# Seven block products in place of eight for two of eight pairs of feature tiles in the down projections

## The chip, the cores and the metric

The kernel runs on one core of a Trainium2 chip. The engines used are TensorE (PE: matmuls, and PEld for the loads of their stationary operand), VectorE (DVE), ScalarE (ACT), GpSimd (POOL, almost idle) and SyncE (SP), whose queue issues the loads of the weights. Each engine works through its own queue in a fixed order, and semaphores hold an instruction back until its inputs are there and its output buffer is free. The metric is the time of one execution on the device in microseconds; less is better.

## What is computed

A two-layer decoder trunk in float32, 256 tokens of 2048 features: a gated short convolution, an MLP, shared keys and values, stick-breaking attention, a second MLP. Only the MLPs matter here; each stands between two norms and is added to the residual:

```python
D_MODEL = 2048; SEQ = 256; D_FF = 4 * D_MODEL

def sq_relu_mlp(u, w_up, w_down):
    return jnp.square(jax.nn.relu(u @ w_up)) @ w_down

def reference(...):
    ...
    u = rmsnorm(h, mlp_pre_g[i])
    h = h + rmsnorm(sq_relu_mlp(u, mlp_w_up[i], mlp_w_down[i]), mlp_post_g[i])
    ...
```

## The kernel before

**Two-part numbers.** TensorE multiplies float32 operands in a rounded format (F32R). To keep accuracy, every operand is split into a high part (the rounded value) and a low part (the rest), and a product is the sum of three matmuls: high x high, high x low of the weights, low of the activations x high (lines 258 to 260). For each weight chunk ACT writes the high part (L149) and DVE the low part (L160; with a gain L162).

**Chunks and buffers.** All weights come as one stream of chunks of 128 x 1024, 512 KB each. `load_one` (L125) issues a chunk's load on SP's queue into one of 4 raw buffers (`RAW`), `split_one` (L177) splits it into a pair of tiles `hi` and `lo`, of which there are rings of 7 each (`RING`), and issues the next load. `chunk(i)` (L187) is called when TensorE's work on chunk i is written down, and sees to it that splits up to `i + 4` (`AHEAD`) are written down first.

**Who sets the order.** TensorE's order is that of the program's text. For DVE and ACT the compiler's planner picks the order: of what is ready it takes the piece of the highest priority, as a rule the one written earlier; `high_priority` puts a piece ahead. Some stretches are ordered by hand for DVE and ACT (`manual_schedule`): the ends of the sub-layers, where a projection's last results pass through the norm into the next sub-layer. They begin with `leave.begin()` in `run` (L293) and end some units later. The class `Norms` and its kinds `KeyNorms` (end of the first MLP) and `OutNorms` (end of the second) say what is done there; the results go through `post`, `gained`, `residual`, `input` and `enter` (transposing on TensorE, L211).

**The MLP** (`mlp`, L774) works in four quarters of the hidden features. A quarter `up(q)` computes 16 feature tiles of 128 x 256 tokens; `hidden` (L778) takes each from PSUM, applies the squared ReLU and splits the tile into high and low (`split_tile`, L201). Up tile n uses PSUM bank `(n + 2) % 8`. Then the quarter's down projection adds its share: two groups j of 1024 output columns each, 16 chunks to a group, one for each of the 16 feature tiles.

**A group** (`Group`, L240) has 2 token blocks b x 2 column halves c, four PSUM banks (2 to 5 for j = 0; 6, 7, 0 and 1 for j = 1). For every chunk `unit(b, i)` issues, for both halves, the three matmuls of 512 columns (`half`, L248): 12 matmuls a chunk. After the last chunk `evict` takes the four banks: in the first quarter a copy on ACT (L854), later a sum on DVE into `part` (L857); in the last quarter `after.post` follows. At the end of an MLP `run` stops the regular order `edge` chunks early (4 for `KeyNorms`, 6 for `OutNorms`), and `last_units` (L270) takes the remaining chunks for one bank after the other, so that the four results come one at a time.

`[P, 512]` scratch comes from `dump` (tag `sq`), gained inputs from the tag `hg` (4 buffers), the gain row of the norm ahead of the MLP from the tag `gpre` (one buffer of 128 x 2048), results from `result` (8 buffers).

Of the kernel before, what the change touches and what calls it, by code (L numbers as in the profile page):

```python
# [9 lines left out]
F32 = mybir.dt.float32  # L10
F32R = mybir.dt.float32r
AF = mybir.ActivationFunctionType
ALU = mybir.AluOpType
# [31 lines left out]
WARM = 8  # L45
LATER = 7
QUARTERS = FF // D

IN_N = [j * KD + i for i in range(KD) for j in range(3)]

# [15 lines left out]
def trunk(ctx, tc, x, xT, vecs, rows, ws, out):  # L66
# [39 lines left out]
    def bank(i, name):  # L106
        return psum.tile([P, 512], F32, tag=f"b{i}", name=name)
# [13 lines left out]
    last_load = [None]  # L121
    count = {"loaded": 0, "split": 0, "limit": 1 << 30, "apart": False}
    lows = []

    def load_one():  # L125
        i = count["loaded"]
# [16 lines left out]
    def high_parts(i):  # L143
        while count["loaded"] <= i:
            load_one()
        hi = wsplit.tile([P, CW], F32R, tag="hi", name=f"whi{i}")
        lo = wsplit.tile([P, CW], F32R, tag="lo", name=f"wlo{i}")
        for j, (at, gain) in enumerate(pieces_of(i)):
            rounded = nc.scalar.activation(  # L149
                hi[:, at], raw[i][:, at], AF.Copy, scale=1.0 if gain is None else gain  # L150
            )
# [14 lines left out]
    def low_parts(until=None):  # L166

        while lows and (until is None or lows[0] <= until):
# [5 lines left out]
            if until is None:  # L174
                break

    def split_one():  # L177
        i = count["split"]
        high_parts(i)
# [60 lines left out]
    class Group:  # L240
# [21 lines left out]
        def unit(self, b, i):  # L262
# [4 lines left out]
                    self.evict(b, c, self.ps.pop((b, c)))  # L267
            spent(UNIT)

        def last_units(self, b, edge):  # L270

            for c in range(2):
                for i in range(self.n - edge, self.n):
                    self.half(b, c, i)
                    if i == self.n - 1:
                        self.evict(b, c, self.ps.pop((b, c)))
                    spent(UNIT / 2)

    def run(groups, enter=False, leave=None):

        units = [(gr, i) for gr in groups for i in range(gr.n)]
        first, last = EDGE if enter else 0, len(units) - (leave.edge if leave else 0)
        for b in range(NB):
            for gr, i in units[:first]:
                gr.unit(b, i)
        for gr, i in units[first:last]:
            if i == 0 and gr.start is not None:
                gr.start()
            for b in range(NB):
                gr.unit(b, i)  # L290
# [465 lines left out]
        y = convolution(tmp)  # L756


    def project(w, xs, n_groups, evict, shift=0):
        groups = []  # L760
        for j in range(n_groups):
            banks = [[(4 * j + 2 * b + c + shift) % 8 for c in range(2)] for b in range(NB)]
# [11 lines left out]
    def mlp(pool, i, before, after):  # L774
        u = before.x4
        part = [[None] * 4 for _ in range(NB)]

        def hidden(xs, n, ps):  # L778
# [9 lines left out]
        def up(q, xs):  # L788
            w = W["up", i, q]
            order = UP_FIRST if q == 0 else UP_ORDER  # L790
            place = {kn: m for m, kn in enumerate(order)}
            pss = {}

            def high(k, n, b=None, begin=True, end=False):

                if n not in pss:
                    pss[n] = bank((n + 2) % 8, "up")
                ps, x = pss[n][:].rearrange("p (a b t) -> p a b t", a=2, b=NB), u[k // 4][:, k % 4]
                if b is None:
                    nc.tensor.matmul(  # L800
                        ps, weight(0, k, n), x, start=begin and k == 0, stop=end and k == KD - 1, skip_group_check=end
                    )
                else:
                    nc.tensor.matmul(ps[:, :, b, :], weight(0, k, n), x[:, :, b, :], start=k == 0 and b == 0, stop=False)  # L804
                if end and k == KD - 1:
                    hidden(xs, n, pss.pop(n))
                spent(TILE_HIGH if b is None else TILE_LOW)

            def low(k, n, begin=False, end=True):
                if n not in pss:  # L810
                    pss[n] = bank((n + 2) % 8, "up")
                x = u[k // 4][:, k % 4, 0].rearrange("p b t -> p (b t)")
                nc.tensor.matmul(  # L813
                    pss[n][:, :T], weight(1, k, n), x, start=begin and k == 0, stop=end and k == KD - 1,
                    skip_group_check=begin,
                )
                if end and k == KD - 1:
                    hidden(xs, n, pss.pop(n))
# [12 lines left out]
            lead = list(range(LEAD_UP if q == 0 else 0))  # L831
            if lead:
                first = [(k, n) for k in range(ALONE) for n in lead]
                for b in range(NB):
                    for k, n in sorted(first, key=lambda kn: (kn[0] // 4, kn[1] // 3 if kn[0] < 4 else 0)):
                        high(k, n, b)
                for k, n in first:
                    low(k, n)
                for k in range(ALONE, KD):
                    tiles_of([(k, n) for n in lead])  # L840
            for n in range(len(lead), KD):
                if n % 2 == 0:
                    tiles_of([(k, n) for k in range(KD)])
                else:
                    for k in range(KD):
                        low(k, n, True, False)
                    for k in range(KD):
                        high(k, n, None, False, True)

        def add(q):  # L850
            def evict(b, c, ps):
                if q == 0:
                    part[b][c] = result()
                    nc.scalar.activation(part[b][c], ps[:], AF.Copy)  # L854
                    return
                with tc.high_priority():
                    nc.vector.tensor_tensor(part[b][c], part[b][c], ps[:], op=ALU.add)  # L857
                if q == QUARTERS - 1:
                    after.post(b, c, part[b][c], part[b][c], before.hs[b][:])
            return evict  # L860

        for q in range(QUARTERS):
            xs = [None] * 4
            up(q, xs)
            if q == QUARTERS - 1:
                turned["banks"] = [2, 3]
            run(project(W["dn", i, q], xs, 2, add(q), 2), leave=after if q == QUARTERS - 1 else None)
# [262 lines left out]
```

## Time and profile before

| | |
|---|---|
| median of 3 runs | 2177.99 us (2177.91 to 2178.13) |
| the profiled execution | 2177.66 us |
| its span, first to last instruction | 2175.9 us |
| mean granted TensorE clock | 0.999 of full |
| busy: PE, PEld, DVE, ACT | 2165.6, 1854.0, 1341.7, 1128.3 us |
| loads of `w_dn` | 256 of 512 KB, 4.0 us to landing |
| first and last matmul of the down projections (L258) | 454.1 and 2166.8 us |

All views come from one profiled execution. The page has the busy time of each engine, the span in 40 slices, the DMA queues, the chain that ended last (followed back from the last instruction to whatever released it), and the costliest groups of instructions. Beside the page the trace answers by line and shape (groups), by who waited for whom (waits), in order of time (timeline; in brackets the engine's idle time before a row and what ended it), and by stage (windows: each engine's busy time in a stretch). Matmuls overlap in the pipeline, so the length of one is not its price; the distance between starts is. L258 is line 258 of the kernel.

### The profile page before, as it was taken

How to read it: one execution, taken by the hardware profiler on the slowest of the kernel's cores; microseconds unless marked ns; L12 is line 12 of the kernel's file. 1: busy time of each engine (PE TensorE's matmuls, PEld its weight loads, DVE VectorE, ACT ScalarE, POOL GpSimd, SP SyncE). 2: the span in 40 equal slices, each digit the busy share in tenths (PEclk: the TensorE clock that was granted, in tenths of full speed). 3: DMA queues.
4: the chain of work that ended last, by engine and by line, in shares of the span. 5: the costliest groups of instructions: out<-in, count | busy, mean ns of one | idle time of the engine just before them, and what ended most of it. 6: DMA issues, size and time to landing. Idle time of an engine off the chain costs nothing.

```text
span 2175.9 us, 28843 instructions
## 1 busy us (share of the span) xinstructions
PE 2165.6 (100%) x11074; PEld 1854.0 (85%) x11074; DVE 1341.7 (62%) x1835; ACT 1128.3 (52%) x1530; POOL 4.4 (0%) x13
## 2 busy tenths in 40 slices
PE   9999999999999999999999999999999999999998
PEld 8888888888888888888888888889888888888886
DVE  8766656854654664565666777558545645655655
ACT  7544444644543453454467888446445434544543
POOL 0000000000000000000000000000000000000000
PEclk9999999999999999999999999999999999999999
DMA  8666575666566666656575546656666666666663
GB/s 304 211 193 193 187 231 165 219 196 193 184 195 193 193 188 195 192 187 185 154 227 163 155 155 208 191 163 220 195 194 186 193 195 192 192 191 193 188 194 116
DMA packets 114762, 417.18 MB, mean 192 GB/s; under 512 B 12864, under 2 KB 13120, under 8 KB 113600
## 3 DMA queue, kind: packets, MB, share of 16 engines
q1 hardware_dynamic: 113472, 408.65, 60.5%
q0 software_dynamic: 864, 6.29, 0.8%
q8 instruction: 87, 1.43, 0.3%
q14 instruction: 51, 0.42, 0.1%
q10 hardware_dynamic: 288, 0.39, 0.1%
HBM read 413.19 MB, written 2.10 MB: 191 GB/s over the span
## 4 chain that ended last, share of the span: by engine, by line
PE 98%; ACT 1%; DMA 0%; DVE 0%; issue 0%; SPq 0%; DVEq 0%; ACTq 0%
PE up L800 20%; PE acc L258 17%; PE acc L260 17%; PE acc L259 17%; PE up L813 11%; PE acc L662 11%; PE lead L662 2%; PE up L804 1%; PE tr L211 1%; PE z L909 0%; PE o L957 0%; ACT whi L149 0%; DMA raw<-w_in 0%; DMA raw<-w_v 0%; ACT L902 0%
## 5 line engine op out<-in xcount | busy, mean ns | idle before, releaser
L160 DVE TENSOR_TENSOR wlo<-raw,whi 128x1024 fp32r<-128x1024 f32 (+1 forms) x678 | 815.7, 1214 | 654.4 <-ACT whi L149 537.8
L149 ACT ACTIVATE whi<-raw 128x1024 fp32r<-128x1024 f32 (+1 forms) x678 | 711.5, 1051 | 642.6 <-PE acc L260 452.9
L800 PE MATMUL up<-u,whi 128*128 128x512 f32 x1952 | 458.3, 390 | 0.0
L800 PEld LDWEIGHTS up<-u,whi 128*128 128x128 f32 x1952 | 361.6, 188 | 71.8
L258 PE MATMUL acc<-whi,hid 128*128 128x512 f32 x1024 | 398.4, 389 | 0.0
L260 PE MATMUL acc<-whi,hid 128*128 128x512 f32 x1024 | 398.4, 389 | 0.0
L259 PE MATMUL acc<-wlo,hid 128*128 128x512 f32 x1024 | 398.3, 389 | 0.0
L813 PEld LDWEIGHTS up<-u,wlo 128*128 128x128 f32 x2048 | 256.0, 191 | 5.8
L813 PE MATMUL up<-u,wlo 128*128 128x256 f32 x2048 | 259.0, 283 | 0.0
L259 PEld LDWEIGHTS acc<-wlo,hid 128*128 128x128 f32 x1024 | 192.2, 188 | 40.0
L260 PEld LDWEIGHTS acc<-whi,hid 128*128 128x128 f32 x1024 | 192.2, 188 | 40.0
L258 PEld LDWEIGHTS acc<-whi,hid 128*128 128x128 f32 x1024 | 192.2, 188 | 39.8
L162 DVE SCALAR_TENSOR_TENSOR wlo<-raw,gv,whi 128x512 fp32r<-128x512 f32 (+1 forms) x160 | 132.1, 854 | 43.7 <-ACT whi L149 43.1
L662 PE MATMUL acc<-u,whi 128*128 128x512 f32 x672 | 156.5, 390 | 0.0
L258 PE MATMUL acc<-whi,u 128*128 128x512 f32 x384 | 153.1, 399 | 0.1
L260 PE MATMUL acc<-whi,u 128*128 128x512 f32 x384 | 149.9, 390 | 0.0
L259 PE MATMUL acc<-wlo,u 128*128 128x512 f32 x384 | 149.7, 390 | 0.0
L149 ACT ACTIVATE whi<-raw,gv 128x512 fp32r<-128x512 f32 (+1 forms) x160 | 121.8, 801 | 51.6 <-PE acc L260 38.9
L662 PEld LDWEIGHTS acc<-u,whi 128*128 128x128 f32 x672 | 124.7, 188 | 25.0
L205 ACT ACTIVATE hid<-s 128x256 fp32r<-128x256 f32 x128 | 52.9, 418 | 106.9 <-DVE s L783 106.4
L780 ACT ACTIVATE half<-up 128x256 f32<-128x256 f32 x128 | 48.3, 382 | 93.2 <-PE up L813 49.2
L260 PEld LDWEIGHTS acc<-whi,u 128*128 128x128 f32 x384 | 72.1, 188 | 15.5
(144 smaller groups left out, 1681.5 us busy)
## 6 DMA issues: line engine op xcount, KB each, us to landing
raw<-w_up SPq DMA_DIRECT2D x256, 512.0 KB, 3.9
raw<-w_dn SPq DMA_DIRECT2D x256, 512.0 KB, 4.0
raw<-w_in SPq DMA_DIRECT2D x94, 512.0 KB, 4.0
raw<-w_out SPq DMA_DIRECT2D x32, 512.0 KB, 4.4
raw<-w_v SPq DMA_DIRECT2D x32, 512.0 KB, 4.4
raw<-w_k SPq DMA_DIRECT2D x32, 512.0 KB, 4.2
raw<-w_q SPq DMA_DIRECT2D x32, 512.0 KB, 4.1
raw<-w_wo SPq DMA_DIRECT2D x32, 512.0 KB, 3.6
```

What stands on the lines that cost most here:

```text
L149: rounded = nc.scalar.activation(hi[:, at], raw[i][:, at], AF.Copy, scale=1.0 if gain is None else gain)
L160: nc.vector.tensor_tensor(lo[:, at], t[:, at], hi[:, at].bitcast(F32), op=ALU.subtract)
L162: nc.vector.scalar_tensor_tensor(lo[:, at], t[:, at], gain, hi[:, at].bitcast(F32), op0=ALU.mult, op1=ALU.subtract)
L205: nc.scalar.activation(hi, src, AF.Copy)
L211: nc.tensor.transpose(to[:, j * P : (j + 1) * P], src[:, j * P : (j + 1) * P], ident[:])
L258: nc.tensor.matmul(ps[:], xh, hi[:, a], start=i == 0 and k == 0, stop=False)
L259: nc.tensor.matmul(ps[:], xh, lo[:, a], start=False, stop=False)
L260: nc.tensor.matmul(ps[:], xl, hi[:, a], start=False, stop=i == self.n - 1 and k == self.ks - 1)
L662: nc.tensor.matmul(ps[:, :cols], w, xs[:, :cols], start=k == 0 and part == parts[0], stop=k == KD - 1 and part == parts[1], skip_group_che ...
L780: nc.scalar.activation(half[:], ps[:, T:], AF.Copy)
L800: nc.tensor.matmul(ps, weight(0, k, n), x, start=begin and k == 0, stop=end and k == KD - 1, skip_group_check=end)
L813: nc.tensor.matmul(pss[n][:, :T], weight(1, k, n), x, start=begin and k == 0, stop=end and k == KD - 1, skip_group_check=begin,)
```

## The change

In each group the feature tiles form eight pairs (0, 1), (2, 3), ..., and for two of them, (2, 3) and (8, 9), the products are formed in another way (`PAIRS`). For a pair the activations are a 2 x 2 block matrix A (two token blocks by two feature tiles), the weights a 2 x 2 block matrix B (two feature tiles by two column halves), and the group needs A B added to its four banks. Before: eight block products, three matmuls each. After: seven block products (Winograd's form of Strassen's method), three matmuls each, whose operands are partly sums: four sums of activations s1 to s4, four of weights t1 to t4. Four of the seven products are added up over both pairs in four further PSUM banks, three go straight to the group's banks; after the second pair the four banks are combined and added to the results.

- `split_seven` takes the place of two splits: four subtractions on DVE, then high and low parts of four tiles in the rings `hi` and `lo` (a: 512 columns, b, t and u: 1024 each).
- `sums_of`, called from `hidden` after tiles 3 and 9, forms s1 to s4 on DVE and splits them; both groups of the quarter use them.
- `Mixed.seven` issues the 21 matmuls; the second tile of a pair issues none.
- `combined` takes the four banks: one copy on ACT and eight sums on DVE; in the first quarter four sums, which start `part`, so that the group's own eviction is a sum on DVE in every quarter.
- The sums of weights and the combining share one buffer under the tag `gpre`; the sums of activations lie under `hg` and `sq`.
- The group's banks stay as they were; the four others are those of the other group of the quarter.

```diff
+PAIRS = (2, 8)
...
+    def split_seven(i):
+
+        while count["loaded"] <= i + 1:
+            load_one()
+        a, b = raw.pop(i), raw.pop(i + 1)
+        sums = sevens[i].tile([P, 4, HALF], F32, tag="gpre", name="sums", bufs=1)
+        t1, t2, t3, t4 = (sums[:, j, :] for j in range(4))
+        b11, b12, b21, b22 = a[:, :HALF], a[:, HALF:], b[:, :HALF], b[:, HALF:]
+        for t, x, y in ((t1, b12, b11), (t3, b22, b12), (t2, b22, t1), (t4, b21, t2)):
+            nc.vector.tensor_tensor(t, x, y, op=ALU.subtract)
+        factors = []
+        for name, src in (("a", b11), ("b", b[:]), ("t", sums[:, 0:2, :]), ("u", sums[:, 2:4, :])):
+            n = 1 if name == "a" else 2
+            src = src if n == 1 or name == "b" else src.rearrange("p a b -> p (a b)")
+            hi = wsplit.tile([P, CW], F32R, tag="hi", name=f"whi{i}{name}")
+            lo = wsplit.tile([P, CW], F32R, tag="lo", name=f"wlo{i}{name}")
+            at = slice(0, n * HALF)
+            nc.scalar.activation(hi[:, at], src, AF.Copy)
+            low_part(hi, lo, src, at, None)
+            factors += [(hi[:, j * HALF : (j + 1) * HALF], lo[:, j * HALF : (j + 1) * HALF]) for j in range(n)]
+        parts[i] = factors
+        count["split"] += 2
+        load_one()
+        load_one()
...
+        def both(self, i):
+            if i in PAIRS:
+                self.seven(i)
+            elif i - 1 not in PAIRS:
+                super().both(i)
+
+        def seven(self, i):
+            b11, b21, b22, t1, t2, t3, t4 = chunk(self.first + i)
+            if self.more is None:
+                self.more = [bank(n, "more") for n in self.extra]
+            sh, sl = self.sums[i]
...
+            p1, p5, p6, p7 = self.more
+            for ps, (xh, xl), (hi, lo), own in (
+                (p1, x(0, 0), b11, True), (self.ps[0, 0], x(1, 0), b21, False), (self.ps[0, 1], sums(3), b22, False),
+                (p5, sums(0), t1, True), (p6, sums(1), t2, True), (p7, sums(2), t3, True),
+                (self.ps[1, 0], x(1, 1), t4, False),
+            ):
+                nc.tensor.matmul(ps[:], xh, hi, start=own and i == PAIRS[0], stop=False)
+                nc.tensor.matmul(ps[:], xh, lo, start=False, stop=False)
+                nc.tensor.matmul(ps[:], xl, hi, start=False, stop=own and i == PAIRS[-1])
+            if i == PAIRS[-1]:
+                self.combine(*self.more)
...
+        def sums_of(x, y):
+
+            t = after.dump()
+            s1, s2, s3, s4 = (t[:, j * P : (j + 1) * P] for j in range(4))
+            a11, a21, a12, a22 = x[:, :P], x[:, P:], y[:, :P], y[:, P:]
+            for to, u, v, op in (
+                (s1, a21, a22, ALU.add), (s2, s1, a11, ALU.subtract),
+                (s3, a11, a21, ALU.subtract), (s4, a12, s2, ALU.subtract),
+            ):
+                nc.vector.tensor_tensor(to, u, v, op=op)
+            hi, lo = (pool.tile([P, 512], F32R, tag="hg", name="sums", bufs=4) for _ in range(2))
+            nc.scalar.activation(hi[:], t[:], AF.Copy)
+            nc.vector.tensor_tensor(lo[:], t[:], hi[:].bitcast(F32), op=ALU.subtract)
+            return hi, lo
...
-                if q == 0:
-                    part[b][c] = result()
-                    nc.scalar.activation(part[b][c], ps[:], AF.Copy)
-                    return
                 with tc.high_priority():
                     nc.vector.tensor_tensor(part[b][c], part[b][c], ps[:], op=ALU.add)
...
+            def combine(p1, p5, p6, p7):
+                w = pool.tile([P, 4, 512], F32, tag="gpre", name="more", bufs=1)
+                t, u2, u3, u4 = (w[:, m, :] for m in range(4))
+                c11, c12, c21, c22 = (part[b][2 * j + c] for b in range(NB) for c in range(2))
+                new = q == 0
...
+                nc.scalar.activation(t, p1[:], AF.Copy)
+                nc.vector.tensor_tensor(u2, t, p6[:], op=ALU.add)
+                nc.vector.tensor_tensor(u3, u2, p7[:], op=ALU.add)
+                nc.vector.tensor_tensor(u4, u2, p5[:], op=ALU.add)
+                if new:
+                    nc.vector.tensor_tensor(c22, u3, p5[:], op=ALU.add)
+                    return
+                nc.vector.tensor_tensor(u2, u3, p5[:], op=ALU.add)
+                for r, v in ((c11, t), (c12, u4), (c21, u3), (c22, u2)):
+                    nc.vector.tensor_tensor(r, r, v, op=ALU.add)
...
+            for j in range(2):
+                ns = [(4 * j + m + 2) % 8 for m in range(8)]
+                groups.append(
+                    Mixed(
+                        w.base + j * KD, xs, [ns[0:2], ns[2:4]], lambda b, c, ps, j=j, q=q: add(q)(b, 2 * j + c, ps),
+                        sums, ns[4:], combined(q, j), pool,
+                    )
+                )
```

More of the change, by code (lines that the diff above doesn't have):

```diff
@@ L123, in trunk @@
     lows = []
+    sevens = {}
     def load_one():
@@ L268, in unit @@
             spent(UNIT)
+        def both(self, i):
+            for b in range(NB):
+                self.unit(b, i)
         def last_units(self, b, edge):
@@ L277, in last_units, with __init__, both, x @@
                     spent(UNIT / 2)
+    class Mixed(Group):
+        def __init__(self, first, xs, banks, evict, sums, extra, combine, pool):
+            super().__init__(first, KD, xs, banks, evict)
+            self.sums, self.extra, self.combine = sums, extra, combine
+            self.more = None
+            for i in PAIRS:
+                sevens[first + i] = pool
+        def both(self, i):
+            if i in PAIRS:
[7 more added lines that the diff above has]
+            sh, sl = self.sums[i]
+            def x(k, b):
+                return [part_of(self.xs, i + k, b, j) for j in range(2)]
+            def sums(j):
+                return [t[:, j * P : (j + 1) * P] for t in (sh, sl)]
+            p1, p5, p6, p7 = self.more
[9 more added lines that the diff above has]
+                self.combine(*self.more)
+            spent(UNIT * 7 / 4)
+            spent(UNIT * 7 / 4)
     def run(groups, enter=False, leave=None):
@@ L288, in run @@
                 gr.start()
-            for b in range(NB):
-                gr.unit(b, i)
+            gr.both(i)
         if leave:
@@ L756, in trunk, with project @@
         y = convolution(tmp)
-    def project(w, xs, n_groups, evict, shift=0):
+    def project(w, xs, n_groups, evict):
         groups = []
         for j in range(n_groups):
-            banks = [[(4 * j + 2 * b + c + shift) % 8 for c in range(2)] for b in range(NB)]
+            banks = [[(4 * j + 2 * b + c) % 8 for c in range(2)] for b in range(NB)]
             groups.append(
@@ L776, in mlp, with hidden @@
         part = [[None] * 4 for _ in range(NB)]
-        def hidden(xs, n, ps):
+        held = {}
+        def hidden(xs, n, ps, sums):
             half = pool.tile([P, T], F32, tag="half", name="half", bufs=2)
@@ L805, in high @@
                 if end and k == KD - 1:
-                    hidden(xs, n, pss.pop(n))
+                    hidden(xs, n, pss.pop(n), sums)
                 spent(TILE_HIGH if b is None else TILE_LOW)
@@ L817, in low @@
                 if end and k == KD - 1:
-                    hidden(xs, n, pss.pop(n))
+                    hidden(xs, n, pss.pop(n), sums)
                 spent(TILE_LOW)
@@ L860, in add, with combined @@
             return evict
-        for q in range(QUARTERS):
-            xs = [None] * 4
-            up(q, xs)
+        def combined(q, j):
+            def combine(p1, p5, p6, p7):
[4 more added lines that the diff above has]
+                if new:
+                    t, u4, u3, c22 = (result() for _ in range(4))
+                    for m, r in enumerate((t, u4, u3, c22)):
+                        part[m // 2][2 * j + m % 2] = r
+                nc.scalar.activation(t, p1[:], AF.Copy)
+                nc.vector.tensor_tensor(u2, t, p6[:], op=ALU.add)
+                nc.vector.tensor_tensor(u3, u2, p7[:], op=ALU.add)
+                nc.vector.tensor_tensor(u4, u2, p5[:], op=ALU.add)
+                if new:
+                    nc.vector.tensor_tensor(c22, u3, p5[:], op=ALU.add)
+                    return
+                nc.vector.tensor_tensor(u2, u3, p5[:], op=ALU.add)
+                for r, v in ((c11, t), (c12, u4), (c21, u3), (c22, u2)):
+                    nc.vector.tensor_tensor(r, r, v, op=ALU.add)
+            return combine
+        for q in range(QUARTERS):
+            xs, sums = [None] * 4, {}
+            w = W["dn", i, q]
+            groups = []
+            for j in range(2):
[6 more added lines that the diff above has]
+                )
+            up(q, xs, sums)
             if q == QUARTERS - 1:
                 turned["banks"] = [2, 3]
-            run(project(W["dn", i, q], xs, 2, add(q), 2), leave=after if q == QUARTERS - 1 else None)
+            run(groups, leave=after if q == QUARTERS - 1 else None)
     def sublayer_pool(name, post, pre):
```

8 lines of the change are left out of this document (7 added, 1 removed).

## The prediction

> **What bounds the kernel now.** I read the page first: the busy line, the granted clock, the chain that ended last.
>
> ```profile
> span 2175.9 us, 28843 instructions
> PE 2165.6 (100%) x11074; PEld 1854.0 (85%) x11074; DVE 1341.7 (62%) x1835; ACT 1128.3 (52%) x1530; POOL 4.4 (0%) x13
> ...
> PEclk9999999999999999999999999999999999999999
> ...
> PE 98%; ACT 1%; DMA 0%; DVE 0%; issue 0%; SPq 0%; DVEq 0%; ACTq 0%
> ```
>
> TensorE is busy all the time, at full clock, and 98% of the chain is its own. A matmul that is not issued therefore shortens the kernel by its step, as long as everything else stays hidden. The step comes from the timeline at the end of the last down projection, and the stage table of that projection's two groups confirms it:
>
> ```profile
> 2165.87 0.39 PE L260 MATMUL acc<-whi,hid 128*128 128x512 f32 x1
> 2166.10 0.39 PE L258 MATMUL acc<-whi,hid 128*128 128x512 f32 x1
> ...
> 2167.23 0.39 PE L260 MATMUL acc<-whi,hid 128*128 128x512 f32 x1
> ```
>
> ```profile
> core 0: us, PE busy (x) PEld busy (x) DVE busy (x) ACT busy (x) POOL busy (x), PEclk, DMA share, GB/s
> 2080.42:2123.94 43.52, 43.52 (x194) 36.04 (x192) 22.09 (x22) 18.48 (x20) 0.00 (x0) 1.00 0.64 192
> 2123.94:2167.46 43.52, 43.52 (x193) 35.85 (x191) 24.44 (x34) 15.59 (x23) 0.00 (x0) 1.00 0.33 111
> ```
>
> 0.39 us is the pipelined length; the starts lie 1.36 us apart for six, so a step is 0.2267 us. A group of 16 chunks x 12 matmuls is 192 steps = 43.52 us, exactly the window, and a chunk is 2.72 us. DVE is busy for 22.1 us of a group and ACT for 18.5: about half.
>
> How far ACT and DVE run ahead is seen in the same stage (ACT, then DVE):
>
> ```profile
> 2118.70 1.06 ACT L149 ACTIVATE whi<-raw 128x1024 fp32r<-128x1024 f32 x1 [1.66 <-PE acc L260]
> 2121.42 1.06 ACT L149 ACTIVATE whi<-raw 128x1024 fp32r<-128x1024 f32 x1 [1.66 <-PE acc L260]
> ```
>
> ```profile
> 2119.79 1.23 DVE L160 TENSOR_TENSOR wlo<-raw,whi 128x1024 fp32r<-128x1024 f32 x1 [1.50 <-ACT whi L149]
> ...
> 2122.10 0.69 DVE L857 TENSOR_TENSOR mg<-mg,acc 128x512 f32<-128x512 f32 x1 [1.08 <-PE acc L260]
> 2122.70 1.22 DVE L160 TENSOR_TENSOR wlo<-raw,whi 128x1024 fp32r<-128x1024 f32 x1
> ```
>
> ACT starts each split when TensorE lets a ring slot go. Chunk 13 ends at 2080.42 + 14 x 2.72 = 2118.50, and ACT starts at 2118.70: that is chunk 20, seven slots on. So a split is made seven chunks (19 us) ahead of its use. It also runs before the eviction of L857, although the text issues chunk 20 only after it: the order on a queue follows what is ready, not the text.
>
> **The change, part by part.**
>
> *Removed.* Each of 2 layers x 4 quarters x 2 groups has two pairs, 32 in all; a pair issues 21 matmuls in place of 24. 96 x 0.2267 = **21.76 us** off TensorE; a pair takes 4.76 us and a group 42.16. [...]
>
> *Added on DVE and ACT.* The prices, from the groups by line and shape:
>
> ```profile
> L160 DVE TENSOR_TENSOR wlo<-raw,whi 128x1024 fp32r<-128x1024 f32 x670 | 812.8, 1224 | 653.4 <-ACT whi L149 536.9 <-issue 96.8 <-PE acc L662 12.7
> L149 ACT ACTIVATE whi<-raw 128x1024 fp32r<-128x1024 f32 x670 | 708.6, 1059 | 641.5 <-PE acc L260 452.9 <-PE up L800 102.8 <-PE acc L662 34.7
> ...
> L857 DVE TENSOR_TENSOR mg<-mg,acc 128x512 f32<-128x512 f32 x48 | 31.3, 683 | 19.1 <-PE acc L260 19.0
> ...
> L440 DVE TENSOR_TENSOR hg<-h,gpre 128x512 f32<-128x512 f32 x16 | 11.0, 689 | 0.4
> ...
> L854 ACT ACTIVATE mg<-acc 128x512 f32<-128x512 f32 x16 | 9.0, 590 | 0.4
> L948 DVE TENSOR_TENSOR lb<-lb,ey 128x128 f32<-128x128 f32 x32 | 9.0, 280 | 0.0
> ```
>
> - Weights of a pair: four subtractions 128x512 from SBUF (as L440) 2.76, and low parts of 512 + 3 x 1024 columns, 0.69 + 3.67: 7.1 us of DVE where two plain splits took 2.4. ACT 3.5 x 1.06 = 3.7 in place of 2.1.
> - Combining, once a group: one ACT copy 0.6 and eight DVE sums of 0.68, 5.5 us (four in the first quarter).
> - Sums of activations, per pair and quarter: 4 x 0.28 + 0.69 = 1.8 us of DVE and 0.6 of ACT, in the up projection, where 88 us leave DVE 32 idle:
>
> ```profile
> 1992.00:2080.00 88.00, 88.00 (x510) 77.97 (x509) 56.08 (x80) 44.91 (x62) 0.00 (x0) 1.00 0.61 191
> ```
>
> A group asks 22.1 - 4 x 1.22 + 14.2 + 5.5 = 36.9 us of DVE in 42.16: 88%, still under the bound, so the question is when each piece is due. In ring entries a group is now 0, 1, a b t u, 4-7, a b t u, 10-15 (pieces of a pair a, b, t, u). Times from the group's start: the last piece of the second pair takes the slot of chunk 4, free at 12.9, done at about 15.2 and 2.3 us of DVE queue allowed, 17.5; its first use is at 21.1 + 3.4 = 24.5. The last piece of the next group's first pair takes chunk 14's slot, free at 39.4, and with four evictions (2.7 us) around it is done by 45; used at 42.2 + 8.8 = 51. The combining starts when product five is done (24.5) and ends at about 30; chunk 14, whose low part then waits behind it, is due at 36.7. The least margin is 6 us, so inside the groups I cost all of this at **nothing**. If that cover went, each pair would cost up to 7.1 - 4.8 = 2.3 us.
>
> *Banks.* The four extra banks are those that the neighbouring group leaves; it evicts by 45, they are opened at 47.6. The sums of weights and the combining share one buffer (that of the gain row, read before the MLP starts): the combining leaves it at 30, the next sums start after 31. Cost nothing.
>
> *Loads.* As many as before:
>
> ```profile
> raw<-w_dn SPq DMA_DIRECT2D x256, 512.0 KB, 4.0
> ```
>
> Both raw buffers of a pair come free after its low parts, some 4 us later than one by one; a load lands in 4.0 us, the use is over 10 us off. SP's queue holds nothing else there, and POOL's gain rows are issued before the MLPs and are not moved. Cost nothing.
>
> *The end of the kernel.* Here the cover is thin. From chunk 10 the last group (edge 6) runs one bank at a time, so it eats a chunk each 0.68 us. Let E be the second pair's end. The combining, ready at E - 1.4, starts behind chunk 13's low part at E - 0.9 and holds DVE to E + 4.6. If chunks 14 and 15 queue behind it (their text is later), their low parts are ready at E + 5.85 and E + 7.1; they are due at E + 2.95 and, after that wait, E + 6.5. TensorE waits 2.9 + 0.6 = **3.5 us**. Bounds: 0 if both low parts go first, 4.7 if chunk 13's also stands behind (it is issued inside the hand-ordered stretch). No trace of before shows the order; I take 3.5, since the combining's text is earlier and both are ready.
>
> *The end of the first MLP* (edge 4) has two whole chunks more: chunk 15 is ready at E + 7.3 and due at E + 7.7. But chunks 16 to 18 then finish at E + 8.5 to 11.1, and the first eviction is due at E + 8.2.
>
> ```profile
> 1059.51 1.28 DVE L162 SCALAR_TENSOR_TENSOR wlo<-raw,gv,whi 128x1024 fp32r<-128x1024 f32 x1 [1.44 <-ACT whi L149]
> 1061.04 0.69 DVE L857 TENSOR_TENSOR mg<-mg,acc 128x512 f32<-128x512 f32 x1 [0.25 <-PE acc L260]
> ```
>
> ```profile
> 1075.53 1.32 DVE mg L366 x2
> 1076.85 0.67 DVE h L430
> 1077.66 0.63 PE tr L211 x4
> ```
>
> The eviction used to follow with 0.25 us to spare, and the chain passes from DVE to TensorE at 1077.66, so lateness on DVE can become a wait. It has high priority, so it is late by at most one split, 0.3 to 1.2; behind all three 2.9. I take 0.4.
>
> **Sum.** The profiled execution took 2177.66 us (1.8 around its span): 2177.66 - 21.76 + 3.5 + 0.4 = 2159.8. The median is 0.33 above that execution, so **2160.0**.
>
> **Rivals.**
>
> 1. *All hidden*: the low parts of chunks 14 and 15 go ahead of the combining. For: ready-first order, as at L857. Against: at E - 0.9 both are ready. Then 2178.0 - 21.8 = 2156.2.
>
> 2. *The clock drops in the last wait.* After TensorE's last matmul the stage table shows
>
> ```profile
> 2164.00:2168.00 4.00, 3.62 (x16) 2.65 (x15) 2.47 (x7) 0.82 (x2) 0.00 (x0) 1.00 0.52 194
> 2168.00:2172.00 4.00, 0.00 (x0) 0.00 (x0) 3.45 (x7) 1.11 (x3) 0.00 (x0) 0.79 0.15 54
> 2172.00:2176.00 4.00, 0.00 (x0) 0.00 (x0) 0.68 (x2) 0.00 (x0) 0.00 (x0) 0.50 0.59 208
> ```
>
> 0.79 is 58% at full and 42% at half clock: it halved at about 2170.3, 2.9 us after the end. A wait of 2.9 to 3.6 us could do the same, and 13 us of matmuls follow. If half clock held for as long again, 3 us, it costs 1.5; for all of it, 13. Time 2161.5 to 2173. [...]
>
> 3. *Small waits at every pair or group*: pieces arrive some 0.2 us late per pair, 6 us; 2164 to 2173.
>
> 4. *The look-ahead runs out (slower).* One pair holds four of seven slots and DVE is at 88%; if DVE, in its fixed order, blocks on a slot with due work behind it, TensorE follows DVE's 7.1 us per pair. It decides at 0.68 us a pair (21.76/32), and with 0.82 the kernel is over 0.2% slower. In full: 32 x 2.3 = 74 us, 2178.0 - 21.8 + 74 + 4 = 2234. Against it: the 6 us of margin above. For it: the margins assume that slots are handed out in order.
>
> That the change issues no fewer matmuls I give nothing: the seven products are listed one by one.
>
> **How the numbers follow.** Forecast (2158 to 2163) 0.48; all hidden 0.28; clock drop 0.06; small waits 0.08; gain used up, within 0.2% (4.4 us, about what a measurement of this kernel can tell from no change), 0.04; slower 0.06. Faster 0.90, same 0.04, slower 0.06. The range runs from 2155.2 (all hidden with 1 us of luck) to 2168 (both ends at their upper bounds, 4.7 + 2.9, and the clock or half of the small waits): about 0.84.
>
> **What would show it.** Groups of 42.16 us with no waits, 96 fewer matmuls with the same 0.2267 us step, DVE at some 36 us per group and, with 16 x 14.8 for the groups and 16 x 1.8 for the sums, at 1342 + 266 = 1608 us or 74% of the span; in the last group, a TensorE wait for a low part (wlo) a few us after the second pair, with the combining's sums on DVE just before. Wrong would be: waits at the pairs (rival 4), DVE ahead by less than 3 us at a pair's first product, or no wait at the end (rival 1).

## The result, and the profile after

| | before | after |
|---|---|---|
| median of 4 runs each, side by side | 2177.95 us | 2161.16 us (2160.87 to 2162.72) |
| ratio, 95% interval | | 0.9924 [0.9907, 0.9941] |
| the profiled execution, its span | 2177.66, 2175.9 us | 2160.87, 2159.2 us |

The change makes the kernel 0.76% faster, 16.8 us; the forecast was 2160.0 us. Of the 21.76 us that TensorE no longer spends, some 5 us came back somewhere. From the page of the changed kernel, the span, the busy line and the chain that ended last:

```profile
span 2159.2 us, 29200 instructions
...
PE 2144.5 (99%) x10978; PEld 1835.9 (85%) x10978; DVE 1563.8 (72%) x2235; ACT 1184.5 (55%) x1610; POOL 4.4 (0%) x13
...
PE 97%; ACT 1%; DVE 1%; DMA 1%; issue 0%; SPq 0%; DVEq 0%; ACTq 0%
```

The number of matmuls fell from 11074 to 10978, by the 96 of the forecast, and TensorE is still nearly the whole chain, 97%. DVE went up by 222 us of busy time.

**Where the saving was made.** Two stretches of the chain of waits around the first quarter's down projection, before and then after (start, length, what): the last piece of one up projection and the first of the next. Between them lie the two groups.

```profile
450.63 3.65 PE up L800 x16
...
541.32 3.63 PE up L800 x16
```

```profile
450.98 3.65 PE up L903 x16
...
538.95 3.63 PE up L903 x16
```

Start to start it was 90.69 us and is 87.97: 2.72 less, which is 12 matmuls of 0.2267 us, three for each of four pairs. The stage table of the changed kernel shows two inner groups, and the last group of the kernel below them (columns as in the prediction):

```profile
1717.51:1759.67 42.16, 42.16 (x187) 34.91 (x187) 34.52 (x42) 21.21 (x23) 0.00 (x0) 1.00 0.61 199
1759.67:1801.83 42.16, 42.16 (x187) 34.91 (x187) 32.39 (x37) 20.86 (x21) 0.00 (x0) 1.00 0.63 202
...
2106.15:2148.31 42.16, 39.88 (x176) 32.70 (x175) 34.28 (x47) 19.37 (x28) 0.00 (x0) 1.00 0.33 116
```

An inner group takes 42.16 us, and TensorE is busy for every one of them. In the last group it is idle for 2.28.

**Where 5 us were lost.** TensorE's waits in the changed kernel (us in total, times, longest):

```profile
PE acc L289 <- DVE wlo L162: 2.3, 1, 2.3
PE tr L241 <- ACT tk L1110: 1.7, 1, 1.7
PE warm L735 <- DVE ones L84: 1.1, 1, 1.1
PE lead L745 <- ACT whi L151: 0.6, 2, 0.4
PE tr L241 <- DVE h L513: 0.3, 1, 0.3
```

Compared stage by stage with the trace of before, the stretch ahead of the first MLP lost 0.33 us, the attention sub-layer between the MLPs 2.03, and the second MLP 2.68. The first MLP, its end among them, lost nothing. The two large rows of the table are new, and they are two different things.

*The last group.* DVE's timeline there (start, length, what):

```profile
2129.51 0.69 DVE L981 TENSOR_TENSOR mg<-mg,more 128x512 f32<-128x512 f32 x1
2130.11 1.22 DVE L162 TENSOR_TENSOR wlo<-raw,whi 128x1024 fp32r<-128x1024 f32 x1
2131.25 0.68 DVE L973 TENSOR_TENSOR more<-more 128x512 f32<-128x512 f32 x1
2131.85 1.22 DVE L162 TENSOR_TENSOR wlo<-raw,whi 128x1024 fp32r<-128x1024 f32 x1
2132.98 0.68 DVE L974 TENSOR_TENSOR more<-more 128x512 f32<-128x512 f32 x1
...
2135.38 1.29 DVE L981 TENSOR_TENSOR mg<-mg,more 128x512 f32<-128x512 f32 x2
2136.58 1.22 DVE L162 TENSOR_TENSOR wlo<-raw,whi 128x1024 fp32r<-128x1024 f32 x1
```

The three subtractions L162 are the low parts of chunks 13, 14 and 15; L973 to L981 are the combining. The high part of chunk 15, ACT's share, starts when its load has landed:

```profile
2131.85 1.06 ACT L151 ACTIVATE whi<-raw 128x1024 fp32r<-128x1024 f32 x1 [1.12 <-DMA raw<-w_dn]
```

It is ready at 2132.9, when DVE has just taken L974. Six sums go by before the low part follows, at 2136.58. TensorE waits for it:

```profile
2135.19 0.39 PE L288 MATMUL acc<-whi,hid 128*128 128x512 f32 x1
2137.86 0.50 PE L289 MATMUL acc<-wlo,hid 128*128 128x512 f32 x1 [2.28 <-DVE wlo L162]
```

From start to start that is 2.67 us in place of 0.23, so 2.44 us are lost at this point.

*The attention.* ACT's timeline, before and then after (in brackets the idle time and what ended it):

```profile
1314.05 1.16 ACT L149 ACTIVATE whi<-raw,gv 128x1024 fp32r<-128x1024 f32 x1
1315.22 1.28 ACT L902 ACT_TABLE_LOAD   x1
1316.52 0.69 ACT L978 ACTIVATE tk<-acc,rq 128x512 f32<-128x512 f32 x1
```

```profile
1305.59 1.16 ACT L151 ACTIVATE whi<-raw,gv 128x1024 fp32r<-128x1024 f32 x1 [2.24 <-DMA raw<-w_v]
1306.76 1.28 ACT L1034 ACT_TABLE_LOAD   x1
1308.06 0.69 ACT L1110 ACTIVATE tk<-acc,rq 128x512 f32<-128x512 f32 x1
```

After is 10.5 us earlier by then (the first MLP's half of the saving, 10.88, less what was lost at the start), so the row at 1314.05 should stand at 1303.55. It stands 2.04 us later, behind a load of `w_v`; the table load and `tk` follow in ACT's order, and TensorE's transposes wait for `tk`. The change touches none of these instructions. The chain of waits gives this load 6.76 us from issue to landing:

```profile
1298.75 6.76 DMA raw<-w_v
```

So the theory was: the changed kernel is the full saving, 2156.2 us, with 2.3 to 2.7 us lost in the last group by the order on DVE (caused by the change), and about 2 us by a late load (not caused by it, or caused by the shift of everything behind it). The rival was that DVE, with 222 us more work, also costs something inside the groups.

### The profile page after: what moved, and what is told of

The parts are those of the page before. It is cut to its first block, busy times and chain, and to the rows that moved or that the text cites. A ratio compares the mean times of both kernels' runs of the same rounds, so it can differ in the third digit from the quotient of the medians.

```text
span 2159.2 us, 29200 instructions
## 1 busy us (share of the span) xinstructions
PE 2144.5 (99%) x10978; PEld 1835.9 (85%) x10978; DVE 1563.8 (72%) x2235; ACT 1184.5 (55%) x1610; POOL 4.4 (0%) x13
## 4 chain that ended last, share of the span: by engine, by line
PE 97%; ACT 1%; DVE 1%; DMA 1%; issue 0%; SPq 0%; DVEq 0%; ACTq 0%
PE up L903 21%; PE acc L288 14%; PE acc L289 14%; PE acc L290 14%; PE up L916 11%; PE acc L745 11%; PE lead L745 2%; PE more L356 1%; PE more L355 1%; PE more L357 1%; PE up L907 1%; PE acc L356 1%; PE acc L355 1%; PE acc L357 1%; PE tr L241 1%
## 5 line engine op out<-in xcount | busy, mean ns | idle before, releaser
L162 DVE TENSOR_TENSOR wlo<-raw,whi 128x1024 fp32r<-128x1024 f32 (+1 forms) x614 | 734.6, 1212 | 365.7 <-ACT whi L151 286.8
L151 ACT ACTIVATE whi<-raw 128x1024 fp32r<-128x1024 f32 (+1 forms) x614 | 639.6, 1051 | 440.4 <-PE acc L290 227.7
L289 PE MATMUL acc<-wlo,hid 128*128 128x512 f32 x768 | 298.9, 389 | 2.3 <-DVE wlo L162 2.3
L288 PE MATMUL acc<-whi,hid 128*128 128x512 f32 x768 | 298.8, 389 | 0.0
L290 PE MATMUL acc<-whi,hid 128*128 128x512 f32 x768 | 298.8, 389 | 0.0
L289 PEld LDWEIGHTS acc<-wlo,hid 128*128 128x128 f32 x768 | 144.1, 188 | 32.5 <-DVE wlo L162 2.7
L290 PEld LDWEIGHTS acc<-whi,hid 128*128 128x128 f32 x768 | 144.2, 188 | 29.9
L288 PEld LDWEIGHTS acc<-whi,hid 128*128 128x128 f32 x768 | 144.1, 188 | 29.9
```

The source lines that it names most:

```text
L151: rounded = nc.scalar.activation(hi[:, at], raw[i][:, at], AF.Copy, scale=1.0 if gain is None else gain)
L162: nc.vector.tensor_tensor(lo[:, at], t[:, at], hi[:, at].bitcast(F32), op=ALU.subtract)
L288: nc.tensor.matmul(ps[:], xh, hi[:, a], start=i == 0 and k == 0, stop=False)
L289: nc.tensor.matmul(ps[:], xh, lo[:, a], start=False, stop=False)
L290: nc.tensor.matmul(ps[:], xl, hi[:, a], start=False, stop=i == self.n - 1 and k == self.ks - 1)
```

## The experiments

**The saving alone.** On the kernel before, the last block product of two chunks in each group is left out, so the output lacks it, the count of matmuls falls as in the change, and nothing is added.

```diff
         def half(self, b, c, i):
             hi, lo = chunk(self.first + i)
+            if self.short and i in (3, 9) and (b, c) == (1, 1):
+                return
```

> The kernel before with 21 matmuls issued for each of the 32 pairs and nothing else changed (one of the eight block products of a pair is left out, so the output lacks it). Theory: the saving is 96 steps of 0.2267 us and nothing is lost inside the groups, so 2177.95 - 21.76 = 2156.2 us, with groups of 42.84 us (a chunk of each pair has 9 matmuls). The 5.0 us that the changed kernel lies above that are 2.3 at the end of the last group, 2.0 in the attention stage and 0.7 in small pieces. If the 2.0 in the attention also stand here, they are not work of the change and the time is about 2158. Rival: the 5 us are a price of the added work spread over the groups; then this shows 2156.2 too, but the groups of the changed kernel would be longer than 42.16, which its trace speaks against; or the saving itself is smaller than the steps say, and this lands at 2160 or above.

2156.92 us, ratio 0.9903 [0.9888, 0.9918]. A group takes 42.16 us (the 42.84 expected counted one pair; two pairs with three matmuls fewer each make 42.16) and keeps DVE's old load:

```profile
1717.50:1759.66 42.16, 42.16 (x187) 34.92 (x187) 22.12 (x22) 17.45 (x18) 0.00 (x0) 1.00 0.71 202
```

DVE's 22.12 here against 34.52 in the change, with the same 42.16: all that the change adds to DVE inside a group is hidden. What it does lose, 2161.16 - 2156.92 = 4.2 us, lies elsewhere.

**The second pair of the last quarter earlier.** The pairs (2, 6) in place of (2, 8) in the last quarter of the second MLP, so that the last group's combining comes before the hand-ordered end.

```diff
+            pairs = (2, 6) if i == 1 and q == QUARTERS - 1 else PAIRS
```

> The changed kernel with the second pair of the last quarter of the second MLP at tiles 6 and 7 instead of 8 and 9, so that the combining starts 5.4 us earlier. Theory (chunk 15's low part stands behind the combining's sums): DVE is done with the combining before chunk 15's low part is ready, TensorE's wait of 2.3 us for a low part is gone, 2161.2 - 2.3 = 2158.9 us. Rival (the load of chunk 15 is late by itself): the wait stays at about 2 us, 2161.2.

2156.87 us, ratio 0.9904 [0.9889, 0.9918]. The row for `wlo` is gone from the table of waits. It came out below the 2158.9 expected, since the load of `w_v` was on time as well (4.51 us): the late load, which I had taken as fixed in the changed program, was not there.

**The last split ahead of the combining.** Nothing is moved on TensorE; in the last group the splits that remain are written ahead of the combining, in the text and so in priority.

```diff
             if i == PAIRS[-1]:
+                if self.first + KD == len(stream):
+                    chunk(self.first + KD - 1 - AHEAD)
                 self.combine(*self.more)
```

> The changed kernel with the splits of the last group's chunks 13 to 15 written down ahead of the combining. Theory (order on the queue): chunk 15's low part runs as soon as its high part is there, which in the changed kernel was 3.7 us before DVE came to it; the wait of 2.3 us is gone or under 0.3, 2158.9 us; the combining ends one split later, which the first eviction, 0.8 us of idle time behind it, can just take. Rival (late load): the wait stays, 2161.2.

2156.74 us (2155.91 to 2159.79), ratio 0.9904 [0.9890, 0.9919]. DVE's timeline at the same place:

```profile
2129.90 1.22 DVE L162 TENSOR_TENSOR wlo<-raw,whi 128x1024 fp32r<-128x1024 f32 x1
2131.56 1.23 DVE L162 TENSOR_TENSOR wlo<-raw,whi 128x1024 fp32r<-128x1024 f32 x1 [0.45 <-ACT whi L151]
2132.70 0.68 DVE L975 TENSOR_TENSOR more<-more 128x512 f32<-128x512 f32 x1
```

The low part of chunk 15 starts at 2131.56 in place of 2136.58, before the rest of the combining; TensorE has no wait for it, and the sums are late for nobody. The same work in another order is worth 2161.16 - 2156.74 = 4.4 us between the medians, more than the wait. The rest is the clock and the late load, which this execution did not have; both are taken up below.

**Three pairs in each group.** `PAIRS = (2, 5, 8)`: 48 more matmuls go, 10.9 us, and DVE gets half as many pairs again. (The tag `hg` needs 6 buffers for this, and `half` gives one up.)

```diff
-PAIRS = (2, 8)
+PAIRS = (2, 5, 8)
```

> Three pairs in place of two (tiles 2, 5 and 8 begin them), two more buffers for the sums of activations, one buffer fewer for the up projection's halves. Theory (the groups hide the added work with room to spare): DVE is busy for 34.5 us of a 42.16 us group; a third pair adds about 4.4 and makes 38.9 of 41.48, so the groups last 41.48 us without waits and the time is 2161.2 - 10.9 = 2150.3 us. Rival (the look-ahead is nearly used up: a pair holds four of seven ring slots): TensorE waits at the pairs, some 0.3 us or more for each of 48, and the time is 2160 to 2190.

2150.90 us, ratio 0.9875 [0.9858, 0.9891]: 10.3 us faster than two pairs. The load of `w_v` was on time (5.25 us). The stage table has an inner group, and the table of waits the one at the end:

```profile
1537.83:1579.31 41.48, 41.48 (x184) 34.35 (x184) 36.18 (x44) 22.81 (x25) 0.00 (x0) 1.00 0.66 203
```

```profile
PE acc L289 <- DVE wlo L162: 3.4, 1, 3.4
```

A group is 0.68 us shorter, three matmuls, and still without a wait; DVE is at 36.18 of 41.48, where 38.9 was expected. The wait at the end is 3.4 us, and the granted clock is half for 3.4 us behind it.

**Three pairs, with the last split first.** Both edits.

> Three pairs, and the splits of the last group's chunks 13 to 15 written down ahead of the combining. Theory (order on the queue): the wait of 3.4 us for a low part in the last group of the kernel with three pairs goes, 2150.9 - 3.4 = 2147.5 us, faster than all kernels so far. Rival (with three pairs DVE has too much to do there in any order): a wait of 1 us or more stays, 2148.5 to 2151.

2146.46 us, ratio 0.9856 [0.9838, 0.9873], the fastest of all: 31.5 us below the kernel before. The wait is gone from the table, with it the half clock, and the load was on time in both profiled executions (5.25 and 4.91 us): so the order is worth 2150.90 - 2146.46 = 4.4 us here, the wait and what the clock makes of it. The third pair alone, with the last split first in both kernels, is worth 2156.74 - 2146.46 = 10.3 us.

**More work for DVE at each pair.** The first subtraction of each pair is done four times, then nine times: 3 or 8 operations more, which start 0.60 us apart, 1.8 or 4.8 us per pair. What is computed stays the same.

```diff
-        for t, x, y in ((t1, b12, b11), (t3, b22, b12), (t2, b22, t1), (t4, b21, t2)):
+        for t, x, y in ((t1, b12, b11),) * 4 + ((t3, b22, b12), (t2, b22, t1), (t4, b21, t2)):
```

> The changed kernel with the first subtraction of each pair done four times, that is three more DVE operations of 0.6 to 0.69 us for each of 32 pairs. Theory (6 us of margin at a pair): DVE is busy for 34.5 + 6 x 0.6 = 38 us of a 42.16 us group, the groups stay at 42.16 us; 2159 to 2162 us. Rival (the look-ahead is nearly used up): 2 us more at each pair show as waits, 32 x 1 to 2 = 30 to 60 us more.

> The same with the first subtraction done nine times, eight more operations for each pair. Theory (DVE's sum over a group is the bound, not the single pair): 34.5 + 16 x 0.6 = 44.1 us of DVE do not fit into 42.16; the groups last 44 to 45 us, 16 x 2 to 3 = 30 to 45 us more than the changed kernel, 2191 to 2206 us, slower than before. Rival (the up projections between give DVE time to catch up, so that it is late only at a few pairs): under 2175 us.

2166.41 us with 3 more, outside what was expected, and 2195.76 with 8 more (one execution of each). From the stage table, an inner group with 3 more:

```profile
1546.01:1588.17 42.16, 42.16 (x188) 34.91 (x187) 36.25 (x44) 21.00 (x23) 0.00 (x0) 1.00 0.66 200
```

With 8 more, two quarters of the first MLP (both groups of each), and TensorE's waits in the first of these two:

```profile
629.88:716.60 86.72, 84.88 (x374) 69.77 (x372) 78.93 (x98) 39.01 (x42) 0.00 (x0) 1.00 0.54 184
805.50:893.99 88.49, 86.24 (x373) 70.77 (x372) 80.10 (x100) 40.10 (x43) 0.00 (x0) 0.98 0.55 185
```

```profile
PE more L355 <- ACT whi248t L196: 1.1, 1, 1.1
PE more L356 <- DVE wlo248t L162: 0.8, 1, 0.8
```

With 1.8 us more per pair the groups keep their 42.16 us. The 5 us of that run lie where nothing was expected of the edit: its wait at the end is 3.2 us and half clock follows for 6.8 us, and behind the late load, which came here too (6.83 us, and a wait of 1.8), the clock halves for another 3.4.

With 4.8 us more per pair the kernel is slower than before. The time falls in the range of the theory, 2191 to 2206 us, but the loss is not spread over the groups as the theory had it. In the six quarters that do not end an MLP, TensorE is late at the last of the four pairs alone (chunk 248 is the last pair of the quarter at 629.88), as the experiment's rival said, and these quarters take 85.1 to 86.7 us in place of 84.32. One takes 88.5; there the clock halved too, for some 3.5 us by its row, 0.98 of full. Together that is 13.5 us. Another 22 us were lost in the two quarters that end an MLP, which take 93.3 and 97.7 us in place of 82.3 and 86.9: with waits at more than one pair, waits for the last splits, and a lower clock (0.996 of full over the whole run, against 0.999 in the changed kernel). So this is the mechanism of the slower rival, DVE late with the pieces of a pair, and it sets in between 1.8 and 4.8 us per pair. By rate alone: DVE is busy for 34.52 + 32.39 = 66.9 us of a quarter's 84.32 in the changed kernel, so 17.4 are free, and four pairs ask for 19.2 more, 1.8 too much; the five of the six quarters without half clock lost 0.8 to 2.4. But DVE still idles for 7.8 us of the quarter at 629.88, so the ring's slots may have a share in it; that was not separated.

**The changed kernel again, unchanged; and with two blank lines in the text,** which alter no instruction: what do the late load and the clock do in other executions?

> The changed kernel once more, unaltered. The runs of the kernels with the last quarter's order altered came out 4.3 us under it, of which their traces lay 2.3 to the end of the last group and 1.7 to 2.0 to one load in the attention stage, 20 stages earlier, that landed after 4.5 to 4.8 us instead of 6.8. Theory (the late landing is chance of that set of runs, not the change): this comes out at 2159 to 2159.5, with a landing of about 5 us and a wait of 2.3 us in the last group. Rival (it belongs to the changed kernel): 2161.2 again, landing 6.8.

> The changed kernel with two empty lines in its text, so that the same instructions carry other line numbers. Up to the attention stage the instruction streams of all engines are the same in the changed kernel and in the kernels whose last quarter was altered, yet one load of w_v landed after 6.8 and 7.0 us in the two profiles of the first and after 4.5 and 4.8 in those of the second. Theory (chance of each execution): about 5 us, no wait there, 2159 us where the clock holds. Rival (it stays with the changed program, for a reason that its streams up to there do not show): 6.5 to 7 us again, a wait of about 2, 2161 us.

2162.82 us (2160.26 to 2163.69) and 2161.06 us (2158.81 to 2161.94); ratios 0.9929 [0.9914, 0.9945] and 0.9918 [0.9903, 0.9932]. In both, the wait of 2.3 in the last group and the late load (7.01 and 6.84 us) are there. The repeat was expected at 2159 to 2159.5 us and the shifted text at about 2159 if the late load was chance; both forecasts missed, since the load was late again. New is the clock. TensorE's timeline of the unchanged repeat in the last group, then its stage table by 2 us, where the eighth column is the granted clock:

```profile
2139.05 0.80 PE L289 MATMUL acc<-wlo,hid 128*128 128x512 f32 x1 [2.27 <-DVE wlo L162]
...
2140.07 0.63 PE L288 MATMUL acc<-whi,hid 128*128 128x512 f32 x1
2140.50 0.63 PE L289 MATMUL acc<-wlo,hid 128*128 128x512 f32 x1
...
2142.57 0.39 PE L288 MATMUL acc<-whi,hid 128*128 128x512 f32 x1
2142.80 0.39 PE L289 MATMUL acc<-wlo,hid 128*128 128x512 f32 x1
```

```profile
2138.00:2140.00 2.00, 0.95 (x2) 0.83 (x3) 1.00 (x1) 0.00 (x0) 0.00 (x0) 0.77 0.00 0
2140.00:2142.00 2.00, 2.00 (x6) 1.54 (x5) 1.55 (x4) 0.82 (x2) 0.00 (x0) 0.50 0.00 0
2142.00:2144.00 2.00, 2.00 (x9) 1.61 (x9) 0.28 (x2) 0.00 (x0) 0.00 (x0) 0.88 0.00 0
```

After the wait the matmuls start 0.43 us apart, then 0.23 again. 0.77 is 46% at half clock, 0.92 us; then all 2 us; then 0.88, 24%, 0.48 us: 3.4 us at half clock in all, beginning with the first matmul after the wait. In 3.4 us 7.9 steps of 0.43 fit, 1.8 us worth of work, so it costs 1.6. In the first profiled execution, of the same program with a wait of 2.28 us that ends at 2137.86, the clock stays full:

```profile
2137.00:2139.00 2.00, 1.15 (x5) 0.97 (x6) 1.17 (x2) 0.00 (x0) 0.00 (x0) 1.00 0.00 0
2139.00:2141.00 2.00, 2.00 (x11) 1.65 (x10) 1.45 (x5) 0.82 (x2) 0.00 (x0) 1.00 0.00 0
```

In the execution with the blank lines the clock drops behind its wait of 2.3 us as in the repeat: 0.53 in the 2 us from 2138 and 0.62 in the next two, 3.4 us at half clock. So a wait of 2.3 us was followed by half clock in two executions of three; what tells them apart was not shown. In the profiled executions of the kernels without the wait (pairs (2, 6), and the last split first with two and with three pairs) the clock in the last group is 1.00 up to the last matmul.

**The last split first, again.** Is the late load a property of the changed program?

> The kernel with the splits of the last group's chunks ahead of the combining, once more. Theory (chance of each execution): landing and wait vary, 2156.5 to 2159. Rival (it stays with the program): landing under 5 us, no wait, 2156.7 us.

2157.10 us (2156.81 to 2158.45), ratio 0.9901 [0.9884, 0.9917]. The chain of waits of this run, and of the first run of the same kernel, names the same load:

```profile
1298.97 6.71 DMA raw<-w_v
```

```profile
1299.41 4.80 DMA raw<-w_v
```

One kernel, 6.71 us in one execution and 4.80 in another; with the first TensorE waits 1.9 us for `tk`, with the second 0.2. So the order of the last group does not settle whether the load is late. The two executions ran on different chips, but the chip does not settle it either: of the four executions of the later run, all on one chip, the profiled one took 2158.45 us and the other three 2156.81 to 2157.13, which by their times alone (they have no traces) had the load on time. Across the profiled executions of the kernels of this study the same load was late in six (6.3 to 7.0 us) and not in the others (4.5 to 5.3). The six are all five that have two pairs in every group, at (2, 8), and the changed kernel's order at the end, among them the two with added subtractions, and one of the five with other pairs or another order. Whether the program makes the late load more likely therefore stays open, and so does what makes it late; no experiment addressed the memory side, and whether the earlier timetable makes it more frequent than in the kernel before was not tried.

## Why the prediction was right, and where it was not

**The saving: right.** 96 matmuls, 0.2267 us a step, groups of 42.16 us with no wait, confirmed by the groups of the changed kernel and by the saving alone at 2156.92 us against 2156.2 for *all hidden*.

**Nothing inside the groups: right, with DVE priced too high.** A group was to ask 36.9 us of DVE and asked 34.5 and 32.4; the total was to be 1608 us and is 1563.8. The term took the lengths of single operations (0.68, 1.22 us). In the rows of the last group, sums that are queued start 0.60 us apart and a low part gives way after 1.14, because each begins before the one ahead is over; the busy time counts the overlap once. The margins were wider too. The last pieces of the second pair of one group and of the first pair of the next, in the group that starts at 1717.51:

```profile
1731.60 1.23 DVE L162 TENSOR_TENSOR wlo616u<-sums,whi616u 128x1024 fp32r<-128x1024 f32 x1
...
1758.26 1.22 DVE L162 TENSOR_TENSOR wlo626u<-sums,whi626u 128x1024 fp32r<-128x1024 f32 x1
```

They end 15.3 and 42.0 us into the group, where 17.5 and 45 were written, so some 9 us ahead of their use in place of 6. The runs with added subtractions show where it would have ended.

**The end of the kernel: right in kind, too large.** The second pair ends at E = 2131.79, the start of the next matmul. The combining was to run from E - 0.9 to E + 4.6; its first sum went early, at E - 2.3, and the others ran from E - 0.5 to E + 4.9. But the low parts of both chunks 14 and 15 were to stand behind it, 3.5 us, and chunk 14's went in between, at 2131.85; only chunk 15's, whose high part was ready at 2132.9, came behind all. That the text's order decides between ready pieces was the premise; for chunk 15 it held, as the run with the split written first shows, for chunk 14 it did not. The wait is one, of 2.3 us.

**The end of the first MLP: 0.4 was too much.** The eviction comes at 1050.51, with one split behind it and not ahead, and the chain from DVE to TensorE keeps its wait of 0.3. DVE's timeline there:

```profile
1050.51 0.69 DVE L956 TENSOR_TENSOR mg<-mg,acc 128x512 f32<-128x512 f32 x1
1051.11 1.28 DVE L164 SCALAR_TENSOR_TENSOR wlo<-raw,gv,whi 128x1024 fp32r<-128x1024 f32 x1
```

**What the sum left out.** The late load, 2.0 us, and 0.3 at the start: neither had a term. In the profiled execution they made up for what the wait was short of: 2177.66 - 21.76 + 0.33 + 2.03 + 2.68 = 2160.9, against 2159.8 in the prediction. The number was right within 1.2 us partly because two errors of opposite sign met, which is luck. (2159.8 with the 0.33 of the median is 2160.1, written down as 2160.0.) The other three executions behind the median are another mix: their mean clock is 0.998, where the profiled one has 0.999.

**The rivals.** *All hidden* was not the outcome, but it is what the kernel gives as soon as one split is put ahead. *The clock drops* had 0.06 and was too low: it dropped in the last group in two of three profiled executions of this program, and its price, 1.5 us for 3 us of half clock, was about right (1.6 for 3.4). I had reasoned from a halving 2.9 us after the last matmul and a wait of 2.9 to 3.6; the wait that came was shorter, 2.3 us, and half clock followed it in two of the three. The 12 executions of the changed program run from 2158.81 us, which by its time is 2156.2 + 2.6 and none of the rest (it has no trace), to 2163.69, with the late load and two drops, the first of them behind that load. *Small waits at the pairs* did not occur. *The look-ahead runs out* is a real mechanism, between 1.8 and 4.8 us of DVE per pair away.

## What to carry to other kernels

Where one engine is the bound and another has half its time free there, work can be traded at a loss in operations: here 222 us of DVE paid for 21.8 of TensorE, and a third pair in each group paid again. The price then appears where the look-ahead ends, at the last pieces of work: list what is queued on the helping engine there, and put what the bound engine needs next ahead of what is only due at the end (4.4 us with three pairs, for two lines of order). Price operations that are queued back to back by the distance of their starts, and a short wait of TensorE by the wait and by the half clock that may follow it (here 3.4 us of it behind a wait of 2.27, which cost 1.6).

## What the runs showed of the hardware

- After a TensorE wait of 2.27 us in the last group (the unchanged repeat) the granted clock was 0.50 for 3.4 us, and the matmuls started 0.43 us apart in place of 0.23. After one of 2.28 us at the same place of the same program (the first execution) it stayed at 1.00. After 3.4 us (three pairs) it was half for 3.4 us, after 3.2 us (3 more subtractions) for 6.8.
- The same 512 KB load, issued at the same point of the same program, landed after 4.80 us in one execution and 6.71 in another, and with the late one TensorE waited 1.9 us for `tk`, with the other 0.2.
